# Convolution dealt out in program order, and its norm inside the mLSTM output stage

## The chip, the core and the metric

The kernel runs on one core of a Trainium2 chip. The metric is the device time of one launch in microseconds. Engines are named by their work: TensorE (PE in the rows, PEld for its weight loads), VectorE (DVE), ScalarE (ACT), GpSimd (POOL), SyncE (SP, which issues most transfers).

## What is computed

One layer of a diffusion backbone: 1024 latent tokens of width 1024, and 256 context tokens that share its weights. A first sub-layer mixes tokens in two groups of heads, a second one is a mixture of 64 experts. The change touches the first only. Cut to what matters:

```python
hx = modulate(rms_norm(x, g_pre_mix), shift, scale)         # hc likewise, of the context
z = h @ w_in + b_in                                          # q, k, v, o, gates, ga, gb
u = ga * sigmoid(gb)                                         # group B, convolution
hx_m = mlstm_bidir(q, k, v, gates, states_of_context)        # group A, chunks of 128 tokens
a = rms_norm_per_head(hx_m) * norm_g * sigmoid(o)
y = depthwise_conv(u, width=31, along rows of the grid) + conv_b
b = silu(layer_norm(y, ln_g, ln_b))                          # norm over 512 channels
x = x + gate * rms_norm(concat(a, b) @ w_out + b_out, g_post_mix)
x = x + gate2 * rms_norm(moe(modulate(rms_norm(x), ...)), g_post_ffn)
```

## The kernel before

Activations are kept with channels on the partitions: `X` holds 8 blocks of 128 channels by 1024 tokens. The modulated input is held as a high and a low half, `hH` and `hL`, of the same fp32r type, and each weight block likewise, `wfH` and `wfL`. A product is then three matmuls per block of 128 channels (`mm3`, L436 to L438). A split makes the two halves: a cast on ScalarE for the high one (L50) and a subtraction for the low one (L51), on VectorE or, where the call names it, on GpSimd.

The stages of the front, with the times of the profiled execution:

- To 63 us: the adaLN vectors, the modulation, and the first four features (`first`).
- 63 to 133 us: gate features for the convolution's input. `feat(t, j)` is 24 matmuls of 512 columns into a PSUM tile `pf` (4 buffers); `gated` turns two such features into one block of `U`, the first four blocks of `X`. `context` makes the context's sums of squares (L153, tile `va` as scratch) and its modulation between them.
- 133 to 199 us: the value and gate projections, 2 x 10 groups of 24 matmuls of 264 columns into `pv` (4 buffers), each evacuated by two VectorE additions (L348, L351). The weights `wvL` are split on GpSimd.
- 199 to 235 us: key features `kT`, and between them the steps of a generator, `gates`, which makes scans and transposes of the mLSTM's gate values; its last step turns `nata`, `natb` and `natc` into the columns `colW`, `colG` and `colF` by way of a PSUM tile with two buffers.
- 235 to 285 us: the chunk states (`states`), then `conv_norm`, the query features and the output gates (`o`, features 12 to 15), up to 328 us.
- 328 to 409 us: `outputs`, ten steps over eight chunks of 128 tokens. For a chunk: decay matrices (`pM`, ScalarE makes `Dm`), scores (`pQ`, VectorE multiplies `Dm` and `qs`), sums (`pN`, ScalarE copies to `hd`), division (`dn`, `hd`), a norm per head and transposes (`pH`). `filler` steps another generator, `ada`, between them; it computes the remaining adaLN vectors from weights that come by DMA (`wa`, `va`, `kT` as buffers) and splits the output weights (`woL`).
- From 409 us: the output projection, and the experts from about 530 to 1450 us.

The convolution (`conv`, L421 on) is four blocks of 31 VectorE instructions, called taps here: one multiplication by the middle weight (L425) and 30 multiply-adds over shifted rows (L431), each on 128 x 784 to 1008 elements, from `U` into `Y`, the last four blocks of `X`. Before, `later(LOW + 1000 * t)` gives them a low priority, and the scheduler puts them where VectorE has nothing else to do by its estimate. The last block is issued behind the key features.

`conv_norm` (L806 on) runs in two halves of 512 tokens: two additions over the four blocks (L813, L814), a product with ones for the mean (`pmu`, L816), a subtraction over four blocks (L817), squares on ScalarE (L820, L821), two additions (L822, L823), a product for the variance (`pva`, L826), a power on GpSimd (L830), a product that spreads the factor (`crs`, L833) and a multiplication over four blocks (L835). Then, for each block, a sigmoid of the scaled value (ScalarE, L838), the scaling (L839) and the product of both (L840).

The order of the other instructions is the program's, moved by a scheduler with priorities; `behind()` ties an instruction behind the last one issued on an engine.

Of the kernel before, what the change touches and what calls it, by code (L numbers as in the profile page):

```python
# [19 lines left out]
EPS = 1e-6  # L20
# [12 lines left out]
class Layer:  # L33
# [72 lines left out]
    def front(self, cp):  # L106
# [8 lines left out]
        gt = mix.tile([128, 10, 16], F32, name="gt")  # L115
# [199 lines left out]
        for t in range(4):  # L315
            if t in (1, 2):
                with self.behind():
                    context(t - 1)
            if t:
                for f, j in [(8 + t, 0), (8 + t, 1), (4 + t, 0), (4 + t, 1)]:  # L320
                    gated(t, f, j, feat(f, j))
# [62 lines left out]
        self.states(sp, stp, va, kT, cst, colW, acol)  # L384
# [18 lines left out]
        self.outputs(qT, kT, va, cst, colG, colF, rows, U)  # L403
# [17 lines left out]
    def conv(self, u, y, cw, cv):  # L421
        nc = self.nc
        u = u.rearrange("p (r w) -> p r w", w=ROW)
        y = y.rearrange("p (r w) -> p r w", w=ROW)
        nc.vector.tensor_scalar(y, u, cw[:, 15:16], cv[:, 0:1], op0=OP.mult, op1=OP.add)  # L425
        for i in range(CW):
            o = i - 15
            if o == 0:
                continue
            a, b = max(0, -o), min(ROW, ROW - o)  # L430
            nc.vector.scalar_tensor_tensor(y[:, :, a:b], u[:, :, a + o:b + o], cw[:, i:i + 1], y[:, :, a:b],  # L431
                                           op0=OP.mult, op1=OP.add)
# [8 lines left out]
    def gates(self, sp, pp, gt, colG, colF, colW, acol):  # L441
# [79 lines left out]
        for col, src, nm in ((colW, Ws, "a"), (colG, G, "b"), (colF, Fl, "c")):  # L521
            t = sp.tile([NR, 128], F32, name="nat" + nm)
            natural(t, src)
# [45 lines left out]
    def states(self, sp, pp, va, kT, cst, colW, acol):  # L569
# [4 lines left out]
        for c in range(9):  # L574
            for d in range(2):
# [22 lines left out]
                prev[d] = C  # L598

    def outputs(self, qT, kT, va, cst, colG, colF, rows, os):  # L600
# [101 lines left out]
        nxt, last, normed = products(0, decays(0)), None, None  # L702
        for x in range(10):
# [90 lines left out]
    def stage_mix(self, sp, X, j):  # L794
        fH = sp.tile([128, 8, 128], F32R, name="fH")
        fL = sp.tile([128, 8, 128], F32R, name="fL")
# [9 lines left out]
    def conv_norm(self, ys, cv):  # L806
        nc, tc = self.nc, self.tc
        sp, sp_ = self.pool("cn", 1)
        pp, pp_ = self.pool("cnp", 1, PSUM)
        for s in range(2):  # L810
            y = ys[:, :, s * 512:s * 512 + 512]
            a = sp.tile([128, 2, 512], F32, name="csa")
            nc.vector.tensor_tensor(a, y[:, :2], y[:, 2:], op=OP.add)  # L813
            nc.vector.tensor_tensor(a[:, 0], a[:, 0], a[:, 1], op=OP.add)  # L814
            pm = pp.tile([128, 512], F32, name="pmu")
            nc.tensor.matmul(pm, self.ones, a[:, 0], start=True, stop=True)  # L816
            nc.vector.scalar_tensor_tensor(y, pm.unsqueeze(1).to_broadcast([128, 4, 512]), -1.0 / 512, y,  # L817
                                           op0=OP.mult, op1=OP.add)
            sq = sp.tile([128, 2, 512], F32, name="csq")
# [4 lines left out]
            pv = pp.tile([128, 4], F32, name="pva")  # L824
            for j in range(4):
                nc.tensor.matmul(pv[:, j:j + 1], a[:, 0, j * 128:j * 128 + 128], self.ones[:, :1], start=True,  # L826
                                 stop=True)
            rc = sp.tile([128, 4], F32, name="crc", bufs=2)
            nc.vector.tensor_scalar(rc, pv, 1.0 / 512, EPS, op0=OP.mult, op1=OP.add)
            nc.gpsimd.tensor_tensor(rc, rc, self.mhalf[:, :4], op=OP.pow)  # L830
            rs = pp.tile([128, 512], F32, name="crs")
            for j in range(4):
                nc.tensor.matmul(rs[:, j * 128:j * 128 + 128], rc[:, j:j + 1].to_broadcast([128, 128]), self.ident,  # L833
                                 start=True, stop=True)
            nc.vector.tensor_tensor(y, y, rs.unsqueeze(1).to_broadcast([128, 4, 512]), op=OP.mult)  # L835
            for t in range(4):
# [4 lines left out]
        self.close(pp_)  # L841
        self.close(sp_)
# [989 lines left out]
```

## Time and profile before

| | us |
|---|---|
| median of three runs | 1489.70 |
| lowest, highest | 1486.15, 1490.43 |
| the profiled execution | 1489.12 |
| its span | 1487.3 |
| TensorE busy in it | 1414.0 (95%) |
| VectorE busy | 1126.0 (76%) |
| ScalarE busy | 753.6 (51%) |
| GpSimd busy | 482.8 (32%) |

A busy share is an average over stages with different limits, so the rows below are by stretch. A wait is listed as the engine that waited, the tile and line it waited at, and the engine, tile and line that released it. PEclk is the clock that TensorE was granted, as a share of its full one. Durations of consecutive instructions on one engine can overlap by some 70 ns.

### The profile page before, as it was taken

How to read it: one execution, taken by the hardware profiler on the slowest of the kernel's cores; microseconds unless marked ns; L12 is line 12 of the kernel's file. 1: busy time of each engine (PE TensorE's matmuls, PEld its weight loads, DVE VectorE, ACT ScalarE, POOL GpSimd, SP SyncE). 2: the span in 40 equal slices, each digit the busy share in tenths (PEclk: the TensorE clock that was granted, in tenths of full speed). 3: DMA queues.
4: the chain of work that ended last, by engine and by line, in shares of the span. 5: the costliest groups of instructions: out<-in, count | busy, mean ns of one | idle time of the engine just before them, and what ended most of it. 6: DMA issues, size and time to landing. Idle time of an engine off the chain costs nothing. (4 is left out here: it accounts for less than half of the span.)

```text
span 1487.3 us, 22926 instructions
## 1 busy us (share of the span) xinstructions
PE 1414.0 (95%) x8188; PEld 1085.2 (73%) x8195; DVE 1126.0 (76%) x1927; ACT 753.6 (51%) x1241; POOL 482.8 (32%) x322
## 2 busy tenths in 40 slices
PE   6999999998899989999999999999999999999975
PEld 4687987775577755866788888888777777777764
DVE  6899979767767896635578888888786877787636
ACT  4421011245533245535567676676676766676622
POOL 0245101112313331334333233333343354455324
PEclk9999999999999999999999999999999999999988
DMA  8421051018743577996999999999999999999975
GB/s 330 163 72 43 1 193 59 19 55 292 224 175 110 200 271 282 353 284 212 342 298 321 325 327 319 333 339 341 319 340 307 301 349 317 316 352 315 335 249 211
DMA packets 95409, 371.64 MB, mean 250 GB/s; under 512 B 18269, under 2 KB 28837, under 8 KB 68794
## 3 DMA queue, kind: packets, MB, share of 16 engines
q1 hardware_dynamic: 66970, 298.48, 53.7%
q0 software_dynamic: 26032, 70.19, 19.4%
q10 hardware_dynamic: 2288, 1.45, 0.4%
q8 instruction: 66, 1.08, 0.3%
q14 instruction: 53, 0.43, 0.1%
HBM read 322.38 MB, written 62.19 MB: 259 GB/s over the span
## 5 line engine op out<-in xcount | busy, mean ns | idle before, releaser
L51 DVE TENSOR_TENSOR u<-u,u 128x1024 fp32r<-128x1024 f32 x354 | 421.8, 1220 | 124.0 <-ACT u L50 97.3
L50 ACT CAST u<-u 128x1024 fp32r<-128x1024 f32 x354 | 361.3, 1052 | 107.6 <-PE pgu L438 41.6
L1580 POOL DMA_INDIRECT acc<-yb,dst x98 | 192.2, 1961 | 352.8 <-ACT hTH L50 118.4
L436 PE MATMUL pgu<-u,xH 128*128 128x512 f32 x608 | 246.9, 406 | 0.4
L437 PE MATMUL pgu<-u,xH 128*128 128x512 f32 x608 | 239.8, 394 | 0.0
L438 PE MATMUL pgu<-u,xL 128*128 128x512 f32 x608 | 239.2, 393 | 0.0
L1460 POOL DMA_INDIRECT xg<-hxd,tok x98 | 125.1, 1276 | 193.7 <-DVE rwj L1368 67.9
L431 DVE SCALAR_TENSOR_TENSOR X<-X,cw 128x912 f32<-128x912 f32 (+14 forms) x120 | 152.0, 1292 | 1.1
L436 PEld LDWEIGHTS pgu<-u,xH 128*128 128x128 f32 x608 | 115.0, 189 | 25.8 <-ACT u L50 2.6
L438 PEld LDWEIGHTS pgu<-u,xL 128*128 128x128 f32 x608 | 114.9, 189 | 24.9
L437 PEld LDWEIGHTS pgu<-u,xH 128*128 128x128 f32 x608 | 115.1, 189 | 21.7
L436 PE MATMUL py<-u,hTH 128*128 128x512 f32 x304 | 122.3, 402 | 0.5 <-ACT hTH L50 0.5
L437 PE MATMUL py<-u,hTH 128*128 128x512 f32 x304 | 119.9, 394 | 0.0
L438 PE MATMUL py<-u,hTL 128*128 128x512 f32 x304 | 118.6, 395 | 0.0
L437 PE MATMUL pf<-hL,wfH 128*128 128x512 f32 x256 | 103.6, 405 | 0.7 <-DVE hL L226 0.7
L51 DVE TENSOR_TENSOR xL<-px,xH 128x512 fp32r<-128x512 f32 x152 | 97.6, 682 | 7.6 <-ACT xH L50 7.2
L436 PE MATMUL pf<-hH,wfH 128*128 128x512 f32 x256 | 103.0, 406 | 0.0
L438 PE MATMUL pf<-hH,wfL 128*128 128x512 f32 x256 | 102.1, 399 | 0.0
L50 ACT CAST xH<-px 128x512 fp32r<-128x512 f32 x152 | 84.0, 593 | 14.7 <-PE pgu L437 8.7
L51 POOL TENSOR_TENSOR wfL<-wfr,wfH 128x1024 fp32r<-128x1024 f32 x14 | 48.9, 3493 | 117.3 <-ACT wfH L50 103.3
L1572 DVE COPY yb<-py 128x512 f32<-128x512 f32 x75 | 51.6, 688 | 46.3 <-PE py L438 45.8
L1482 PE MATMUL px<-ident,xg 128*128 128x128 f32 x600 | 83.7, 274 | 1.0 <-DVE nl L1265 1.0
(438 smaller groups left out, 2500.2 us busy)
## 6 DMA issues: line engine op xcount, KB each, us to landing
u<-in_we_dram SPq DMA_DIRECT2D x192, 1024.0 KB
wa<-in_wa_dram SPq DMA_DIRECT2D x40, 256.0 KB
wa<-in_wa_dram SPq DMA_DIRECT2D x8, 1024.0 KB
wfr<-in_wf_dram SPq DMA_DIRECT2D x16, 512.0 KB
v<-acc SPq DMA_DIRECT2D x16, 512.0 KB
acc<-zero SPq DMA_DIRECT2D x13, 512.0 KB
u<-in_ws_dram SPq DMA_DIRECT2D x6, 1024.0 KB
X<-in_xT_dram SPq DMA_DIRECT2D x8, 512.0 KB
```

What stands on the lines that cost most here:

```text
L50: self.nc.scalar.copy(H, src)
L51: return (eng or self.nc.vector).tensor_tensor(L, src, H.bitcast(F32), op=OP.subtract).ins
L431: nc.vector.scalar_tensor_tensor(y[:, :, a:b], u[:, :, a + o:b + o], cw[:, i:i + 1], y[:, :, a:b], op0=OP.mult, op1=OP.add)
L436: mm(out, lH, rH, start=start, stop=False, skip_group_check=free)
L437: mm(out, lH, rL, start=False, stop=False, skip_group_check=free)
L438: mm(out, lL, rH, start=False, stop=stop, skip_group_check=free)
L1460: nc.gpsimd.indirect_dma_start(out=x[:n], out_offset=None, in_=self.hx, in_offset=bass.IndirectOffsetOnAxis(ap=self.tok[:n, c:c + 1], axis=0),
L1482: nc.tensor.transpose(pt[:, k], x[:, (4 * q + k) * 128:(4 * q + k) * 128 + 128], self.ident)
L1572: nc.vector.tensor_copy(y[:, 512:], py)
L1580: nc.gpsimd.indirect_dma_start(out=self.acc[b % NA].rearrange("r (n d) -> (r n) d", n=n), in_=y[:rows], in_offset=None, out_offset=bass.In ...
```

## The change

1. **Taps.** `conv` becomes a generator that yields after each tap. A new `spend(n)` takes the next `n` taps of a list of such generators and keeps each in program order. It is called behind every gate feature (4 taps behind a first half; 3 or 2 behind a second), behind every value group (2), behind every key feature (4), behind every state step (1); the rest is spent behind the states.
2. **Splits.** The low halves of `wf` (all but two of its blocks were on GpSimd) and of `wv` are made on VectorE.
3. **PSUM of the value groups.** Odd groups use `pv` (4 buffers), even ones `pf` (4 buffers).
4. **Gates.** The generator yields once more, ahead of the transposes into `colW`, `colG`, `colF`; the first two query features stand ahead of that last step.
5. **The convolution's norm.** It leaves its place between the states and the query features and becomes a generator that `outputs` steps once per chunk, behind `divide(x, 0, pN)`. Chunks 0 and 2 take the sums, the mean and the subtraction of a half; chunks 1 and 3 its squares and variance; chunks 4 and 5 the spread factor and the multiplication; chunk 6 the activation. Its tiles take the buffers `fH` and `fL` that the output projection uses later, its products the PSUM tile `pH`, the factor the tile `gt`.
6. **Swish.** The sigmoid, the scaling and the product are one activation (Silu with scale and bias), four instructions of 128 x 1024, in place. The function table is loaded once more for it.

The diff's core:

```diff
-                self.split(wH, wL, wr, nc.gpsimd if len(wts) > 1 else None)
+                self.split(wH, wL, wr)
...
+        taps = []
+        def spend(n):
+            for _ in range(n):
+                while taps:
+                    ins = next(taps[0], None)
+                    if ins is not None:
+                        tc.keep_in_program_order(ins)
+                        break
+                    taps.pop(0)
+        taps.append(self.conv(U[:, 0], Y[:, 0], cw[:, 0], cv[:, 0]))
-        for t in range(4):
+        for t in range(1, 4):
...
-            if t < 3:
-                with self.later(LOW + 1000 * t):
-                    self.conv(U[:, t], Y[:, t], cw[:, t], cv[:, t])
+            for f, j in [(8 + t, 0), (8 + t, 1), (4 + t, 0), (4 + t, 1)]:
+                gated(t, f, j, feat(f, j))
+                spend((3 if t == 1 else 2) if j else 4)
+            taps.append(self.conv(U[:, t], Y[:, t], cw[:, t], cv[:, t]))
...
-                self.split(wH, wL, wr, nc.gpsimd)
+                self.split(wH, wL, wr)
...
-                ps = pv.tile([128, 264], F32, name="pv", bufs=4)
+                ps = pv.tile([128, 264], F32, name="pv", bufs=4) if j % 2 else pj.tile([128, 512], F32, name="pf", bufs=4)
+                ps = ps[:, :264]
...
+                spend(2)
...
-                if (t, j) >= (0, 2):
+                if (0, 2) <= (t, j) < (1, 2):
                     with self.behind():
                         next(gates, None)
-                    if (t, j) == (0, 2):
-                        with self.behind(mybir.EngineType.DVE), self.later(LOW):
-                            self.conv(U[:, 3], Y[:, 3], cw[:, 3], cv[:, 3])
+                spend(4)
...
+        query(0)
+        with self.behind():
+            next(gates, None)
-        self.states(sp, stp, va, kT, cst, colW, acol)
+        self.states(sp, stp, va, kT, cst, colW, acol, spend)
+        spend(CW * 4)
...
-        self.conv_norm(Y, cv)
-        for t in range(2):
-            for j in range(2):
-                nc.scalar.activation(qT[:, t, j * 512:j * 512 + 512], feat(t, j), AF.Identity, bias=bf[:, t:t + 1])
+        query(1)
...
+        swish = self.conv_norm(sp, pp, ys, cv)
         for x in range(10):
...
                 hs = [divide(x, 0, pN)]
+                next(swish, None)
...
-                g = sp.tile([128, 512], F32, name="csg", bufs=2)
-                nc.scalar.activation(g, y[:, t], AF.Sigmoid, scale=cv[:, t, 1:2], bias=cv[:, t, 2:3])
-                nc.vector.tensor_scalar(y[:, t], y[:, t], cv[:, t, 1:2], cv[:, t, 2:3], op0=OP.mult, op1=OP.add)
-                nc.vector.tensor_tensor(y[:, t], y[:, t], g, op=OP.mult)
+        self.grouped([lambda t=t: nc.scalar.activation(ys[:, t], ys[:, t], AF.Silu, scale=cv[:, t, 1:2],
+                                                       bias=cv[:, t, 2:3]) for t in range(4)])
```

The instructions that move, on VectorE. First where the context's sums (`va`) meet the first taps (`X<-X,cw`), behind the first gate features (`X<-pf,bf,X`). Before:

```order
L431 SCALAR_TENSOR_TENSOR X<-X,cw 128x16x50
L153 TENSOR_TENSOR va<-va 128x256
L431 SCALAR_TENSOR_TENSOR X<-X,cw 128x16x51
L214 TENSOR_SCALAR rc<-pc 128x2
L309 MEMSET va 128x40
```

Now:

```order
L233 SCALAR_TENSOR_TENSOR X<-pf,bf,X 128x512 x2
L153 TENSOR_TENSOR va<-va 128x256 x3
L214 TENSOR_SCALAR rc<-pc 128x2
L309 MEMSET va 128x40
L443 TENSOR_SCALAR X<-X,cw,cv 128x1024
```

The sums stand in one run, ahead of the first instruction of the convolution (L443).

The second place is the end of the gates' generator, where the columns are copied (`colW`, `colG`, `colF`) and the first key block is weighted (`kw`). Before:

```order
L514 TENSOR_SCALAR natc<-Fl 64x128
L515 TENSOR_SCALAR natc<-Fl 40x128
L431 SCALAR_TENSOR_TENSOR X<-X,cw 128x16x59
L526 COPY colW<-pc 128x104
L526 COPY colG<-pc 128x104
L431 SCALAR_TENSOR_TENSOR X<-X,cw 128x16x60
L526 COPY colF<-pc 128x104
L530 COPY acol<-pa 64x52 x2
L431 SCALAR_TENSOR_TENSOR X<-X,cw 128x16x61
L583 TENSOR_TENSOR kw<-pt,colW 128x256 x2
```

Now:

```order
L449 SCALAR_TENSOR_TENSOR X<-X,cw 128x16x53
L449 SCALAR_TENSOR_TENSOR X<-X,cw 128x16x54
L449 SCALAR_TENSOR_TENSOR X<-X,cw 128x16x55
L449 SCALAR_TENSOR_TENSOR X<-X,cw 128x16x56
L547 COPY colW<-pc 128x104
L547 COPY colG<-pc 128x104
L547 COPY colF<-pc 128x104
L51 TENSOR_TENSOR wfL<-wfr,wfH 128x1024
L551 COPY acol<-pa 64x52 x2
L604 TENSOR_TENSOR kw<-pt,colW 128x256 x2
```

Eight taps, four of them shown, now stand between the last row of `natc` and the copies, with a cast, two mask tiles and a split of weights among them; another split (`wfL`) follows the copies.

The third is the first chunk of the output stage, on VectorE. Before:

```order
L650 TENSOR_TENSOR qs_2715<-qT,pQ 128x256
L650 TENSOR_TENSOR qs_2720<-qT,pQ 128x256
L658 TENSOR_TENSOR Dm_2695<-Dm_2695,pQ 128x512
L658 TENSOR_TENSOR Dm_2703<-Dm_2703,pQ 128x512
L51 TENSOR_TENSOR woL<-wor,woH 128x512
L675 TENSOR_TENSOR dn<-hd_2774,colF 128x4
L677 SCALAR_TENSOR_TENSOR dn<-hd_2774,dn 128x4
L678 RECIPROCAL dn<-dn 128x4
L680 TENSOR_TENSOR hd_2774<-hd_2774,dn 128x4x128
```

Now:

```order
L672 TENSOR_TENSOR qs_2625<-qT,pQ 128x256
L843 SCALAR_TENSOR_TENSOR X<-pmu,X 128x4x512
L672 TENSOR_TENSOR qs_2630<-qT,pQ 128x256
L680 TENSOR_TENSOR Dm_2605<-Dm_2605,pQ 128x512
L680 TENSOR_TENSOR Dm_2613<-Dm_2613,pQ 128x512
L51 TENSOR_TENSOR woL<-wor,woH 128x512
L697 TENSOR_TENSOR dn<-hd_2684,colF 128x4
L699 SCALAR_TENSOR_TENSOR dn<-hd_2684,dn 128x4
L700 RECIPROCAL dn<-dn 128x4
```

The subtraction of the convolution's mean (L843) stands between the two multiplications of `qs`.

The last is ScalarE in the seventh chunk, where the decays of the last chunk (`Dm`) are followed by the copies of the sums (`hd<-pN`). Before:

```order
L637 ACTIVATE Dm_3499<-pM,colG 128x128 x4
L637 ACTIVATE Dm_3507<-pM,colG 128x128 x4
L50 CAST woH<-wor 128x512
L761 DMA ga_3686<-in_rows_dram 32x256
L673 COPY hd_3539<-pN 128x516
```

Now:

```order
L659 ACTIVATE Dm_3465<-pM,colG 128x128 x4
L864 ACT_TABLE_LOAD
L864 ACTIVATE X<-X,cv 128x1024 x3
L695 COPY hd_3497<-pN 128x516
L710 ACTIVATE hd_3441,ssq<-hd_3360 128x128 x4
```

The load of the function table and three of the four Silu (L864) stand ahead of the next copy of `hd`.

From the output projection on, the order on every engine is as before.

## Rows read from the trace of the kernel before

**Rows 1.** Windows by stretch: busy us (x instructions) of each engine, granted clock, DMA share.

```profile
63.00:328.20 265.20, 249.41 (x1450) 212.78 (x1449) 236.53 (x341) 55.30 (x80) 65.05 (x28) 0.97 0.18 58
328.20:409.20 81.00, 72.27 (x642) 45.90 (x649) 58.15 (x139) 45.85 (x154) 23.94 (x32) 0.94 0.80 262
530.00:1450.00 920.00, 905.63 (x5083) 687.77 (x5081) 669.74 (x1072) 574.53 (x868) 333.50 (x207) 0.99 0.94 315
```

**Rows 2.** TensorE's waits, 63 to 410 us: total us, times, longest us.

```profile
PE pv L436 <- DVE gt L351: 5.3, 1, 5.3
PE pc L525 <- DVE nata L515: 3.4, 1, 3.4
PE pmu L816 <- issue: 2.1, 1, 2.1
PE pc L213 <- DVE va L153: 2.0, 1, 2.0
PE crs L833 <- POOL crc L830: 2.0, 2, 1.7
...
PE pa L776 <- DMA kT<-in_wa_dram: 1.6, 1, 1.6
```

**Rows 3.** Windows within the value projections.

```profile
150.20:153.40 3.20, 2.87 (x13) 2.90 (x14) 3.20 (x5) 0.00 (x0) 0.00 (x0) 0.50 0.00 0
153.60:157.00 3.40, 3.40 (x30) 3.40 (x29) 3.40 (x8) 0.00 (x0) 0.00 (x0) 1.00 0.02 5
155.00:195.00 40.00, 39.65 (x326) 39.44 (x325) 39.82 (x57) 1.27 (x2) 4.05 (x2) 1.00 0.00 1
```

**Rows 4.** GpSimd's lines, 60 to 330 us: busy us, mean ns.

```profile
L51 POOL TENSOR_TENSOR wfL<-wfr,wfH 128x1024 fp32r<-128x1024 f32 x12 | 44.0, 3668 | 102.0 <-ACT wfH L50 88.0 <-DMA acc<-zero 14.0
```

**Rows 5.** VectorE's timeline in three places: start us, us, line, tile, count.

```profile
77.99 10.00 DVE L431 SCALAR_TENSOR_TENSOR X<-X,cw 128x896 f32<-128x896 f32 x5
...
142.64 5.50 DVE L431 SCALAR_TENSOR_TENSOR X<-X,cw 128x976 f32<-128x976 f32 x5
...
159.11 2.22 DVE L431 SCALAR_TENSOR_TENSOR X<-X,cw 128x928 f32<-128x928 f32 x2
...
161.66 2.21 DVE L431 SCALAR_TENSOR_TENSOR X<-X,cw 128x912 f32<-128x912 f32 x2
```

**Rows 6.** VectorE's lines, 63 to 330 us: busy us, mean ns.

```profile
L431 DVE SCALAR_TENSOR_TENSOR X<-X,cw 128x912 f32<-128x912 f32 (+14 forms) x120 | 152.0, 1292 | 1.1
...
L817 DVE SCALAR_TENSOR_TENSOR X<-pmu,X 128x2048 f32<-128x2048 f32 x2 | 4.6, 2288 | 1.6 <-PE pmu L816 1.6
L835 DVE TENSOR_TENSOR X<-X,crs 128x2048 f32<-128x2048 f32 x2 | 4.6, 2286 | 3.8 <-PE crs L833 3.8
...
L822 DVE TENSOR_TENSOR csa<-csa,csq 128x1024 f32<-128x1024 f32 x2 | 2.4, 1222 | 2.5 <-ACT csq L821 2.5
L813 DVE TENSOR_TENSOR csa<-X 128x1024 f32<-128x1024 f32 x2 | 2.4, 1220 | 0.0
...
L823 DVE TENSOR_TENSOR csa<-csa 128x512 f32<-128x512 f32 x2 | 1.4, 691 | 0.1
L814 DVE TENSOR_TENSOR csa<-csa 128x512 f32<-128x512 f32 x2 | 1.4, 685 | 0.0
```

**Rows 7.** TensorE's lines, 285 to 409 us.

```profile
L816 PE MATMUL pmu<-csa,ones 128*128 128x512 f32 x4 | 2.4, 685 | 2.1 <-issue 2.1
L833 PE MATMUL crs<-ident,crc 128*128 128x128 f32 x16 | 2.3, 288 | 2.0 <-POOL crc L830 2.0
```

**Rows 8.** ScalarE's timeline at the output stage's start and in its seventh chunk.

```profile
328.99 1.28 ACT L637 ACT_TABLE_LOAD   x1 [0.81 <-DVE X L398]
330.29 2.18 ACT L637 ACTIVATE Dm<-pM,colG 128x128 f32<-128x128 f32 x8
...
381.78 0.59 ACT L673 COPY hd<-pN 128x516 f32<-128x516 f32 x1 [3.69 <-PE pM L634]
```

**Rows 9.** ScalarE's line of the norm's squares, 200 to 330 us.

```profile
L820 ACT ACTIVATE csa<-X 128x1024 f32<-128x1024 f32 x2 | 2.1, 1057 | 0.6 <-DVE X L817 0.6
```

More of the change, by code (lines that the diff above doesn't have):

```diff
@@ L114, in front @@
         va = mix.tile([128, 10, NH, DV + 1], F32, name="va")
-        gt = mix.tile([128, 10, 16], F32, name="gt")
+        gt = self.gt = mix.tile([128, 10, 16], F32, name="gt")
         cw = mix.tile([128, 4, CW], F32, name="cw")
@@ L383, in front, with query @@
         qT = mix2.tile([128, 2, NX], F32, name="qT")
-        self.states(sp, stp, va, kT, cst, colW, acol)
+        def query(t):
+            for j in range(2):
+                nc.scalar.activation(qT[:, t, j * 512:j * 512 + 512], feat(t, j), AF.Identity, bias=bf[:, t:t + 1])
+        query(0)
[3 more added lines that the diff above has]
+        spend(CW * 4)
         self.masks(mix2)
@@ L401, in front @@
         self.close(pj_)
-        self.outputs(qT, kT, va, cst, colG, colF, rows, U)
+        self.outputs(qT, kT, va, cst, colG, colF, rows, U, Y, cv)
         self.close(rp_)
@@ L430, in conv @@
             a, b = max(0, -o), min(ROW, ROW - o)
[L431 to L432 removed]
+            yield nc.vector.scalar_tensor_tensor(y[:, :, a:b], u[:, :, a + o:b + o], cw[:, i:i + 1], y[:, :, a:b],
+                                                 op0=OP.mult, op1=OP.add)
     def mm3(self, out, lH, lL, rH, rL, start, stop, free=False):
@@ L520, in gates @@
             nc.sync.dma_start(self.rowd[i], t)
-        for col, src, nm in ((colW, Ws, "a"), (colG, G, "b"), (colF, Fl, "c")):
-            t = sp.tile([NR, 128], F32, name="nat" + nm)
-            natural(t, src)
+        nat = []
+        for src, nm in ((Ws, "a"), (G, "b"), (Fl, "c")):
+            nat.append(sp.tile([NR, 128], F32, name="nat" + nm))
+            natural(nat[-1], src)
+        yield
+        for col, t in zip((colW, colG, colF), nat):
             pc = pp.tile([128, 128], F32, name="pc", tag="s", bufs=2)
@@ L567, in bound_rows, with states @@
         return out
-    def states(self, sp, pp, va, kT, cst, colW, acol):
+    def states(self, sp, pp, va, kT, cst, colW, acol, spend):
         nc = self.nc
@@ L598, in states, with outputs @@
                 prev[d] = C
-    def outputs(self, qT, kT, va, cst, colG, colF, rows, os):
+                spend(1)
+    def outputs(self, qT, kT, va, cst, colG, colF, rows, os, ys, cv):
         nc, tc = self.nc, self.tc
@@ L794, in stage_mix @@
     def stage_mix(self, sp, X, j):
-        fH = sp.tile([128, 8, 128], F32R, name="fH")
-        fL = sp.tile([128, 8, 128], F32R, name="fL")
+        fH = sp.tile([128, 8, 128], F32R, name="fH", tag="fH")
+        fL = sp.tile([128, 8, 128], F32R, name="fL", tag="fL")
         self.split(fH, fL, X[:, :, j * 128:j * 128 + 128])
@@ L804, in project, with conv_norm @@
                 self.mm3(po[:, s], fH[:, k], fL[:, k], *self.wo[k, n], k == 0, k == 7)
[L806 to L812, printed above, removed]
+    def conv_norm(self, sp, pp, ys, cv):
+        nc = self.nc
+        mm = nc.tensor.matmul
+        halves = [ys[:, :, 512 * s:512 * s + 512] for s in range(2)]
+        bank = lambda nm: pp.tile([128, 512], F32, name=nm, tag="pH")
+        rc = self.gt[:, 0, :8].rearrange("p (s j) -> p s j", s=2)
+        for s, y in enumerate(halves):
+            a = self.spa.tile([128, 2, 512], F32, name="csa", tag="fH")
             nc.vector.tensor_tensor(a, y[:, :2], y[:, 2:], op=OP.add)
             nc.vector.tensor_tensor(a[:, 0], a[:, 0], a[:, 1], op=OP.add)
-            pm = pp.tile([128, 512], F32, name="pmu")
-            nc.tensor.matmul(pm, self.ones, a[:, 0], start=True, stop=True)
+            pm = bank("pmu")
+            mm(pm, self.ones, a[:, 0], start=True, stop=True)
             nc.vector.scalar_tensor_tensor(y, pm.unsqueeze(1).to_broadcast([128, 4, 512]), -1.0 / 512, y,
                                            op0=OP.mult, op1=OP.add)
-            sq = sp.tile([128, 2, 512], F32, name="csq")
+            yield
+            sq = self.spa.tile([128, 2, 512], F32, name="csq", tag="fL")
             nc.scalar.activation(a, y[:, :2], AF.Square)
@@ L823, in conv_norm @@
             nc.vector.tensor_tensor(a[:, 0], a[:, 0], a[:, 1], op=OP.add)
-            pv = pp.tile([128, 4], F32, name="pva")
+            pv = bank("pva")
             for j in range(4):
[L826 to L831, printed above, removed]
+                mm(pv[:, j:j + 1], a[:, 0, j * 128:j * 128 + 128], self.ones[:, :1], start=True, stop=True)
+            nc.vector.tensor_scalar(rc[:, s], pv[:, :4], 1.0 / 512, EPS, op0=OP.mult, op1=OP.add)
+            nc.gpsimd.tensor_tensor(rc[:, s], rc[:, s], self.mhalf[:, :4], op=OP.pow)
+            yield
+        for s, y in enumerate(halves):
+            rs = bank("crs")
             for j in range(4):
-                nc.tensor.matmul(rs[:, j * 128:j * 128 + 128], rc[:, j:j + 1].to_broadcast([128, 128]), self.ident,
-                                 start=True, stop=True)
+                mm(rs[:, j * 128:j * 128 + 128], rc[:, s, j:j + 1].to_broadcast([128, 128]), self.ident, start=True,
+                   stop=True)
             nc.vector.tensor_tensor(y, y, rs.unsqueeze(1).to_broadcast([128, 4, 512]), op=OP.mult)
-            for t in range(4):
-                g = sp.tile([128, 512], F32, name="csg", bufs=2)
-                nc.scalar.activation(g, y[:, t], AF.Sigmoid, scale=cv[:, t, 1:2], bias=cv[:, t, 2:3])
-                nc.vector.tensor_scalar(y[:, t], y[:, t], cv[:, t, 1:2], cv[:, t, 2:3], op0=OP.mult, op1=OP.add)
-                nc.vector.tensor_tensor(y[:, t], y[:, t], g, op=OP.mult)
-        self.close(pp_)
-        self.close(sp_)
+            yield
+        self.grouped([lambda t=t: nc.scalar.activation(ys[:, t], ys[:, t], AF.Silu, scale=cv[:, t, 1:2],
+                                                       bias=cv[:, t, 2:3]) for t in range(4)])
 NE, TK, DE = 64, 8, 256
```

5 lines of the change are left out of this document (1 added, 4 removed).

## The prediction

> **What bounds the kernel now.** I read the windows by stretch first, then TensorE's waits, then the lines and rows behind each wait. The windows [rows 1] show three stretches. From 530 to 1450 us, the experts, TensorE is busy 905.63 of 920.00 us. From 63.0 to 328.2, the front after its first loop, it is busy 249.41 of 265.20, and VectorE 236.53. From 328.2 to 409.2, the mLSTM output stage, TensorE is busy 72.27 of 81.00 and VectorE only 58.15. So the time is TensorE's own work plus its holes, and the holes before 409 are where an edit of this kind can act. Their list [rows 2] names VectorE or the convolution's norm behind most of them: 5.3 us on an evacuation of the value projections (gt, L351), 3.4 on the gate rows (nata), 2.1 and 2.0 in the norm (pmu, crs), 2.0 on the context's sums (va, L153). Each of the first three and the last is followed by a stretch at half clock. The one after the 5.3 us hole is shown: PEclk 0.50 from 150.2 to 153.4 with 13 matmuls, against 30 matmuls in the 3.4 us behind it at 1.00 [rows 3]. These are 1.2 and 2.4 GHz. Half the work in 3.2 to 3.4 us means that a hole of this sort costs 1.6 us more than its length.
>
> **The first gate features (63 to 79 us).** Before, the five sums of the context's squares stand between taps on VectorE, and GpSimd runs its splits of weights meanwhile (3668 ns each) [rows 4]. Taps that take 2.22 us for two at 159 take 10.00 us for five at 78 [rows 5], so the sums come late and TensorE waits 2.0 us. In the new order the sums stand in one block ahead of the first tap, and no split runs on GpSimd. I take the wait and its slow clock away: 2.0 + 1.6 = **3.6 us**. What comes late next is the weight splits, now VectorE's: 12 of 128x1024 in this stretch at the 1.22 us of a sum of that shape (L813) [rows 6], 14.6 us, and 8 of half that size, about 5 us by the same row (an estimate). Against these some 20 us stand the taps: 120 take 152.0 us, 1292 ns each [rows 6], and at the undisturbed 1.11 us of [rows 5] they would take 133. So the 20 us added and the 19 us saved nearly cancel. VectorE also loses the norm, so its 236.53 us must still fit into a front some 20 us shorter; they do, with little over.
>
> **The value projections (133 to 199 us).** One group of 24 matmuls takes TensorE 40.00 / 326 x 24 = 2.94 us [rows 3]. Two taps and an evacuation take VectorE 161.66 - 159.11 = 2.55 us [rows 5]. With two taps dealt out per group and eight PSUM buffers for four, VectorE keeps ahead. Before, VectorE ran five taps in a row from 142.64 on, 5.50 us [rows 5], while the four buffers were full; that hole of 5.3 us goes with its clock: 5.3 + 1.6 = **6.9 us**.
>
> **Gates and states (199 to 285 us).** Two query features now stand ahead of the transposes of the gate rows, so the 3.4 us on nata go, with 1.6 of clock: 5.0. A wait is added: the third transpose needs a PSUM buffer that the copy of colW frees, and that copy stands on VectorE behind eight taps, two mask tiles, a cast and a split. That is about 8 x 1.11 + 1.22 + 1 = 11.1 us (the last 1 my estimate from the smaller shapes), against two features on TensorE of about the same length. Queued behind it on TensorE are the rest of the query features and the states' transposes. I take 1.2 us; the ends are 0 and, with taps at 1.29 us, about 3. Net **3.8 us**.
>
> **The convolution's norm leaves the path between states and query features.** Its two waits go, 2.1 + 2.0, and 1.6 us of clock: **5.7 us**. Its matmuls (2.4 us, 2.3 us and sixteen of one column) [rows 7] go into the output stage at the same price, so they cancel. The 8 multiplications by scale and 8 by the sigmoid leave VectorE for good. The front gains 3.6 + 6.9 + 3.8 + 5.7 = **20.0 us**.
>
> **The output stage.** VectorE gets two subtractions and two multiplications over four blocks (2288 and 2286 ns) and the sums (2.4, 2.4, 1.4, 1.4 us in pairs) [rows 6], 16.8 us, of which the first sums, 1.9, run before the stage. It has 81.00 - 58.15 = 22.85 us of idle time, but its queue is in order and the chunk's chain (qs, Dm, dn, hd) runs through it. The ends are 0, all of it in idle time, and 14.9, all of it on the chain. The four long ones, 9.1 us, stand directly between links of that chain; I expose half of them, **4.6 us**, and leave the short sums hidden. On ScalarE, the squares take 4.2 us beside other work. The four Silu of 1024 elements come in the seventh chunk behind a load of the function table. A load took 1.28 us at 328.99, and the next activation began 0.02 us after it [rows 8]. With three Silu at the 1057 ns of a square of that size [rows 9], 4.5 us stand ahead of the next copy of hd. In that place that copy found ScalarE idle for 3.69 us at 381.78 [rows 8], so 0.8 us are left over; the ends are 0 and 4.5. **0.8 us.** Against this the stage's wait for kT's DMA, 1.6 us [rows 2], halves when chunks last longer: -0.8. The stage grows by 4.6 us beside the moved matmuls.
>
> The Trainium skill (ScalarE: Activation LUTs, What ACT_TABLE_LOAD costs) counts a drain of about 1.38 us beside the load of 1283 ns for each change of set. By that the stage would grow by 1.4 us more, an estimate, and the sum would end at 1475.1. No row here shows that drain: the one in [rows 8] goes on at once.
>
> **Sum.** 1489.1 (the profiled execution; its span is 1487.3) - 20.0 + 4.6 = 1473.7. The median of the three runs, 1489.7, lies 0.6 above that execution and the runs span 4.3. I stay with **1473.7**.
>
> **Rivals.** (A) VectorE's queue becomes the bound of the output stage and it is slower. The norm's matmuls stand in TensorE's order among the chunk's products, and each waits for its link on VectorE or ScalarE, so all 14.9 us of VectorE, 4.5 of Silu and 4.2 of squares are exposed: 23.6 against 20.0, **1492.7**. It decides when the holes of that stage grow from 8.7 us to over 28. Against it stand VectorE's idle 22.85 us; for it, that both engines would be over 85% full. (B) The taps in program order hold up what TensorE needs in the front. Eight splits of gate weights stand behind a tap of 1.11 us each, about 9 to 10 us of new holes: 1473.7 + 10 = **1484**. For it speaks that VectorE has little over; against it, the two-tap rhythm of [rows 5], which already keeps pace. (C) The stage takes the norm into its idle time, so neither the 4.6 nor the 0.8 appears: **1468**. (D) The gain is given back among the experts, whose weights come by DMA at a share of 0.94 [rows 1]: **1489**. Against it stands TensorE's busy 98% there, and 0.06 of 920 us, 55 us, in which the transfers could catch up.
>
> **How the numbers follow.** Chances: the forecast 0.50 (1470 to 1479), C 0.19, B 0.16, A 0.08, D 0.05, something else 0.02. The range reaches over C and most of B: 1466 to 1486; A, D and the tail of B stay outside, less than 2 in 10. A difference of 0.3%, 4.5 us, is about what a measurement of this kernel can tell from no change. Below 1485.2 lie the forecast, C and most of B: faster 0.83; within 0.3% D and the rest of B: 0.09; slower A: 0.08.
>
> **What would show it.** The list of TensorE's waits before the output stage should have none of the five named ones over 1.5 us, and PEclk should stay near 1.00 from 63 us to the stage. That stage should begin about 20 us earlier plus the length of the moved matmuls, near 301 to 305 us, and last 88 to 93 us. In it, waits on hd or on the norm's tiles of about 5 us in sum are mine, of 20 are A's. New waits on wfL or pf before 300 would be B's. The experts should take as long as before; if they take longer, D. I would be wrong first on how much of the four 2.29 us instructions the chunk chain feels.

## The result and the profile after

The changed kernel takes 1465.9 us (median of four runs, 1462.6 to 1466.7) against 1489.55 (four runs, 1486.2 to 1490.4). The ratio is 0.9846, with a 95% interval from 0.9827 to 0.9865. It is faster, as forecast, by 23.7 us where 16 were forecast. The time lies on the lower edge of the stated range, 1466 to 1486, 0.1 us below it in the median, and outside the forecast's own 1470 to 1479.

Windows of the changed kernel's profile (1466.07 us; span 1464.3), with the columns of [rows 1], by the same stretches of work: the front, the output stage, 920 us of experts. The columns are the window, its length, the busy us of TensorE, its weight loads, VectorE, ScalarE and GpSimd, the granted clock, the DMA share and GB/s.

```profile
63.00:303.20 240.20, 239.17 (x1426) 205.88 (x1425) 208.05 (x335) 47.37 (x72) 2.58 (x5) 1.00 0.20 64
303.20:388.20 85.00, 75.27 (x678) 49.37 (x684) 71.77 (x153) 55.13 (x163) 29.97 (x34) 0.96 0.76 249
509.00:1429.00 920.00, 906.60 (x5085) 689.07 (x5084) 670.66 (x1070) 573.63 (x867) 332.88 (x208) 0.99 0.94 315
```

In the front TensorE is busy 239.17 of 240.20 us, and its granted clock is 1.00; before it was 249.41 of 265.20 at 0.97 [rows 1]. In the output stage VectorE went from 58.15 of 81.00 us to 71.77 of 85.00. The experts are as before. TensorE's waits of the changed kernel over 63 to 388 us, columns of [rows 2]:

```profile
PE pH L720 <- DVE X L862: 2.9, 1, 2.9
PE pa L800 <- DMA wa<-in_wa_dram: 2.5, 2, 2.3
PE pa L800 <- DMA va<-in_wa_dram: 1.4, 2, 1.2
...
PE pM L653 <- ACT X L414: 0.8, 1, 0.8
```

None of the five named holes of [rows 2] is left. All of the waits shown fall in the output stage; the 0.8 us on pM stand ahead of its first matmul. Where the time went is read from the starts of the same matmuls in both timelines (start, duration): the first feature, the first value group, the output stage (pM), the output projection (po) and the first expert (pgu). First before, then after.

```profile
29.60 0.50 PE L436 MATMUL pf<-hH,wfH 128*128 128x512 f32 x1
...
133.37 0.28 PE L436 MATMUL pv<-wvH,hH 128*128 128x264 f32 x1
...
199.34 0.40 PE L436 MATMUL pf<-hH,wfH 128*128 128x512 f32 x1
...
328.23 0.38 PE L631 MATMUL pM<-cm,idb 128*128 128x512 bf16 x1 [0.78 <-ACT X L397]
...
408.93 0.50 PE L436 MATMUL po<-woH,fH 128*128 128x512 f32 x1
...
531.87 0.59 PE L1492 MATMUL pgu<-u,xR 128*128 128x512 f32 x1
```

```profile
32.55 0.50 PE L454 MATMUL pf<-hH,wfH 128*128 128x512 f32 x1
...
132.82 0.28 PE L454 MATMUL pf<-wvH,hH 128*128 128x264 f32 x1
...
191.26 0.40 PE L454 MATMUL pf<-hH,wfH 128*128 128x512 f32 x1
...
303.16 0.38 PE L653 MATMUL pM<-cm,idb 128*128 128x512 bf16 x1 [0.78 <-ACT X L414]
...
388.17 0.50 PE L454 MATMUL po<-woH,fH 128*128 128x512 f32 x1
...
509.80 0.59 PE L1515 MATMUL pgu<-u,xR 128*128 128x512 f32 x1
```

| stretch | before | after | difference |
|---|---|---|---|
| to the first feature | 29.60 | 32.55 | +2.95 |
| first feature to value groups | 103.77 | 100.27 | -3.5 |
| value groups | 65.97 | 58.44 | -7.5 |
| keys to output stage | 128.89 | 111.90 | -17.0 |
| output stage | 80.70 | 85.01 | +4.3 |
| projection to first expert | 122.94 | 121.63 | -1.3 |
| the rest of the span | 955.4 | 954.5 | -0.9 |

The first line of the table is no part of the change: the first feature starts between 29.6 and 32.6 us in the fourteen profiles, whose kernels differ only behind it. From the first feature to the output stage 28.0 us are gone. Part of that is the norm's matmuls, which went into the stage (2.4, 2.3 and 1.9 us by their busy times before, 6.6 in sum; in a row they take less, since they overlap).

### The profile page after: what moved, and what is told of

It is laid out like the page before. It is cut to its first block, busy times and chain, and to the rows that moved or that the text cites. A ratio compares the mean times of both kernels' runs of the same rounds, so it can differ in the third digit from the quotient of the medians.

```text
span 1464.3 us, 22838 instructions
## 1 busy us (share of the span) xinstructions
PE 1405.1 (96%) x8188; PEld 1080.2 (74%) x8195; DVE 1109.2 (76%) x1933; ACT 753.3 (51%) x1238; POOL 421.5 (29%) x300
## 5 line engine op out<-in xcount | busy, mean ns | idle before, releaser
L449 DVE SCALAR_TENSOR_TENSOR X<-X,cw 128x784 f32<-128x784 f32 (+14 forms) x120 | 137.4, 1145 | 1.6
L455 PE MATMUL pf<-hL,wfH 128*128 128x512 f32 x256 | 100.5, 393 | 0.0
L50 ACT CAST xH<-px 128x512 fp32r<-128x512 f32 x152 | 84.0, 592 | 14.6 <-PE pgu L455 8.7
L1539 ACT ACTIVATE sgu<-pgu 128x256 f32<-128x256 f32 x79 | 30.5, 386 | 103.2 <-PE pgu L456 103.2
```

Of the source, the lines that this page charges most:

```text
L50: self.nc.scalar.copy(H, src)
L449: yield nc.vector.scalar_tensor_tensor(y[:, :, a:b], u[:, :, a + o:b + o], cw[:, i:i + 1], y[:, :, a:b], op0=OP.mult, op1=OP.add)
L455: mm(out, lH, rL, start=False, stop=False, skip_group_check=free)
L1539: nc.scalar.activation(sg, pg[:, :DE], AF.Silu)
```

## Experiments

Times are medians of four or more runs, with the ratio to the kernel before on the same chip and its 95% interval. The chips differ: the kernel before takes 1486.9, 1488.2 and 1489.7 us on the three of the experiments, so between sections the ratios compare better than the times. "Changed" is the changed kernel, 0.9846 (0.9827 to 0.9865).

**Norm back in the front.**

```diff
+        self.conv_norm(Y, cv)          # ahead of query(1), in the form of before
         query(1)
...
-                next(swish, None)
```

> The changed kernel with the convolution's norm back between the states and the second pair of query features, in its old form (sigmoid, scaling, product); everything else as changed. Theory 1 (the output stage takes the norm into its idle time, so that only its matmuls cost there): the two waits and the slow clock come back, about 5.7 us, and the stage falls from 85 to 81 us: about 1471.5. Theory 2 (the forecast's: the four long VectorE instructions and the Silu cost the stage 4.6 us more than the matmuls): about 1467, and the stage falls to 76 to 77 us.

Measured: 1492.5, ratio 1.0018 (1.0001 to 1.0035). Both theories were wrong, by over 20 us. Its waits from 192 to 335 us:

```profile
PE pva L849 <- DVE csa L846: 8.1, 1, 8.1
PE crs L856 <- POOL crc L853: 3.4, 2, 1.7
PE pmu L839 <- DVE csa L837: 2.8, 1, 2.8
PE pmu L839 <- issue: 2.8, 1, 2.8
PE pM L654 <- DVE X L858: 2.4, 1, 2.4
...
317.00:339.00 22.00, 9.78 (x49) 6.17 (x52) 17.39 (x25) 9.43 (x13) 1.40 (x1) 0.50 0.48 169
```

The norm's chain is exposed for 19.5 us, and in all of 317 to 339 us, where the hole of 8.1 us lies, the granted clock is 0.50 and TensorE is busy 9.78 of 22.00 us. Both theories had priced the norm's return by the waits of the kernel before, which are not those of this front. The output stage itself is 82.7 us here.

**Norm alone moved, the rest as before.**

```diff
 # the kernel before, with only:
-        self.conv_norm(Y, cv)          # ahead of the query features
...
+                next(swish, None)      # in the output stage, with Silu
```

> The kernel before with only the norm moved into the output stage and its sigmoid replaced by Silu. Theory 1: the front loses the waits pmu and crs and one slow stretch, 5.7 us, and the stage grows by the matmuls it takes over: about 1484, with the waits on the value projections (5.3) and on nata (3.4) still there. Theory 2: 4.6 us of it are lost again in the stage: about 1488.5.

Measured: 1481.2, 0.9945 (0.9926 to 0.9965): 8.5 us gained, more than theory 1 said. Its stage is 83.6 us with the norm, 80.7 before without: the 2.9 us are less than the matmuls' 6.6. The stretch from the keys to the stage takes 117.0 us (201.16 to 318.18), 11.9 less than before. The holes on gt, nata (3.4) and va (2.0) are still there:

```profile
PE pv L435 <- DVE gt L351: 6.4, 1, 6.4
```

**Splits back on GpSimd.**

```diff
-                self.split(wH, wL, wr)
+                self.split(wH, wL, wr, nc.gpsimd if len(wts) > 1 else None)
...
-                self.split(wH, wL, wr)
+                self.split(wH, wL, wr, nc.gpsimd)
```

> The changed kernel with the low halves of the front's weights split on GpSimd again. If GpSimd's splits stretched the taps beside them, the 120 taps take 150 us again instead of 137, about 13 us more, while VectorE loses 20 us of splits; TensorE then waits again in the first gate features, about 2 us with 1.6 of slow clock: about 1469 to 1470. If it was the order alone (sums ahead of the taps) that took the wait away: no change, 1466, with the taps slower all the same.

Measured: 1470.9, 0.9884 (0.9856 to 0.9911), 5.0 us above changed. The size was right and the place was not: there is no wait on va, the taps take 1329 ns each, and TensorE waits later, where the gates end:

```profile
PE pc L546 <- DVE colW L547: 5.4, 1, 5.4
```

**Four buffers for the value groups.**

```diff
-                ps = pv.tile([128, 264], F32, name="pv", bufs=4) if j % 2 else pj.tile([128, 512], F32, name="pf", bufs=4)
-                ps = ps[:, :264]
+                ps = pv.tile([128, 264], F32, name="pv", bufs=4)
```

> The changed kernel with all value groups in the four buffers of pv. If the second set of buffers is what removed the 5.3 us hole, a hole of 3 to 5 us with its slow clock comes back: 1470 to 1473. If dealing the taps out two per group is enough by itself: 1466, and no wait over 1 us in the value projections.

Measured: 1467.6, 0.9862 (0.9837 to 0.9887), not told apart from changed. The value groups take the same 58.3 us from first to last matmul and have no wait.

**Last step of the gates ahead of the query features.**

```diff
-        query(0)
         with self.behind():
             next(gates, None)
+        query(0)
```

> The changed kernel with the last step of the gates (the transposes of nata, natb, natc) ahead of the first two query features again. If those features are what covers the wait on nata, a hole of about 3.4 us with 1.6 us of slow clock comes back: about 1471. If the dealt-out taps already let VectorE reach nata in time: about 1466, with no wait over 1 us at the transposes.

Measured: 1466.0, 0.9854 (0.9817 to 0.9892): no change. The waits at the transposes are small without the cover:

```profile
PE pc L546 <- DVE colW L547: 0.9, 1, 0.9
```

**Taps as low-priority fill again.**

```diff
-                        tc.keep_in_program_order(ins)
...
+        def low(t):
+            with self.later(LOW + 1000 * t):
+                list(self.conv(U[:, t], Y[:, t], cw[:, t], cv[:, t]))
...
-            taps.append(self.conv(U[:, t], Y[:, t], cw[:, t], cv[:, t]))
+            if t < 3:                  # the last block behind the key features, as before
+                low(t)
```

> The changed kernel with the convolution's instructions as low-priority fill again, as before, instead of dealt out in program order; splits on VectorE, eight buffers, the order of the gates and the norm in the output stage stay. If dealing out is what removes the holes: the 5.3 us hole of the value projections comes back, smaller for the second set of buffers, and the context's sums stand between taps again, 2.0 us, each with its slow clock: 1472 to 1478. If the splits' new engine and the buffers did it: 1466 to 1468.

Measured: 1465.8, 0.9850 (0.9818 to 0.9882). Dealing the taps out gains nothing in this kernel; no wait on va or gt came back.

**Fill and four buffers together.** Both edits above.

> Two parts undone at once: the convolution's instructions are low-priority fill again, and all value groups use the four buffers of pv; splits on VectorE, the order of the gates and the norm's place stay. Undone singly, neither brought the hole of the value projections back. If each of the two removes it by itself, it comes back here, 4 to 6 us and 1.6 of slow clock: 1471 to 1474. If neither matters and it was the splits on GpSimd that caused it: 1465 to 1467.

Measured: 1464.3, 0.9838 (0.9813 to 0.9862). The second expectation held, to 0.7 us (1465 to 1467 was said): neither matters while the splits are on VectorE. Fill, four buffers and GpSimd's splits were together in the kernel with the norm alone moved, which has the 6.4 us hole; here there is none in the value groups.

**Fill and GpSimd's splits together.**

> Two others undone at once: low-priority fill, and the splits on GpSimd; eight buffers, the order of the gates and the norm's place stay. If GpSimd's splits caused the holes of the front where the taps are fill: the wait of 2.0 us on va and its slow clock come back, and one of some us in the value projections: 1471 to 1476. If eight buffers cover that: about 1471, as with the splits alone undone.

Measured: 1480.7 (1475.1 to 1484.5), 0.9938 (0.9918 to 0.9958), 13 us by the ratios above the same kernel with the splits on VectorE (16 above the one with four buffers, measured on the same chip), and above the 1471 to 1476 that was expected. Eight buffers keep the value groups free of a long hole, though the splits are on GpSimd and the taps are fill; the delay turns up around them, at the context's sums, at the padded gates and at their columns:

```profile
PE pc L553 <- DVE colW L554: 4.8, 1, 4.8
PE pg L490 <- DVE pad L482: 2.7, 1, 2.7
PE pc L213 <- DVE va L153: 2.0, 1, 2.0
...
PE pf L462 <- POOL wvL L51: 0.7, 1, 0.7
```

Behind the waits on pad and colW the matmuls run at half clock again (0.50 from 213.9 to 217.0 us); behind the one on va the granted clock is 1.00 (74.9 to 78.3).

**Norm back in the front, taps as fill.**

> The norm back in the front in its old form, and the taps as low-priority fill; splits on VectorE, eight buffers and the order of the gates stay. If dealing out is what made the norm's return cost 26 us (the last tap comes late, and the norm's chain behind it finds no features left to cover it), this kernel is at 1471 to 1476. If the chain is exposed because the shortened front and the early query features leave too little to cover it, wherever the taps stand: 1485 to 1493.

Measured: 1475.05, 0.9904 (0.9880 to 0.9928): 17 us below the first experiment, which differs in the dealing-out alone, and within the 1471 to 1476 of its first expectation. The longest waits:

```profile
PE crs L863 <- POOL crc L860: 2.4, 2, 1.7
PE pmu L846 <- issue: 2.4, 1, 2.4
```

The norm's first sum (csa, line of before L813) starts at 281.96 us here and at 296.00 with the taps dealt out. VectorE's timeline of both, around the last tap; first as fill, then dealt out:

```profile
267.55 0.48 DVE L583 MEMSET rw<- 80x512 f32 x1
...
274.48 1.03 DVE L457 SCALAR_TENSOR_TENSOR X<-X,cw 128x784 f32<-128x784 f32 x1
...
281.51 0.42 DVE L579 TENSOR_TENSOR rwR<-rw,rwR 32x256 fp32r<-32x256 f32 x1 [4.74 <-ACT rwR L578]
281.96 1.22 DVE L843 TENSOR_TENSOR csa<-X 128x1024 f32<-128x1024 f32 x1
...
281.58 0.48 DVE L576 MEMSET rw<- 80x512 f32 x1
...
286.07 1.03 DVE L450 SCALAR_TENSOR_TENSOR X<-X,cw 128x784 f32<-128x784 f32 x1
...
295.54 0.42 DVE L572 TENSOR_TENSOR rwR<-rw,rwR 32x256 fp32r<-32x256 f32 x1 [4.75 <-ACT rwR L571]
296.00 1.23 DVE L836 TENSOR_TENSOR csa<-X 128x1024 f32<-128x1024 f32 x1
```

The sum does not start behind the last tap, which ends 6.5 and 8.9 us earlier. It starts behind the split of two tiles of rows that the kernel reads back from memory (rwR), and that waits 4.7 us in both kernels for ScalarE's copy, which waits for a DMA into rw (3.7 and 5.0 us). The first of these transfers is issued behind the clearing of rw on VectorE (268.1 and 282.1 us), and the clearing stands among the taps: dealt out, it comes 14.0 us later, as the sum does. A kernel with the norm ahead of these rows was not run.

**Six more long VectorE instructions in the output stage.**

```diff
                 next(swish, None)
+                if x < 6:
+                    e = ys[:, :, 512:] if x in (0, 1, 4) else ys[:, :, :512]
+                    nc.vector.scalar_tensor_tensor(e, e, 1.0, e, op0=OP.mult, op1=OP.max)
```

> The changed kernel with one more VectorE instruction over 128 x 4 x 512 elements, about 2.3 us, in each of the first six chunks of the output stage: it multiplies a half of the convolution's result by 1 and changes nothing; 13.7 us in all. Theory 1 (VectorE has room in the stage): the stage grows by at most 3 us beyond 85, and the time is under 1469. Theory 2 (half of a long instruction is felt): 6.9 us, 1473. Rival A of the prediction (the chunk's chain feels all of it): 13 to 14 us, 1479 to 1480.

Measured: 1475.2 (runs from 1466.7 to 1480.7), 0.9916 (0.9885 to 0.9948): 9.3 us above changed. In the profile the stage grows from 85.0 to 91.0 us. Its window:

```profile
301.70:392.70 91.00, 77.18 (x679) 49.46 (x684) 82.51 (x156) 54.68 (x162) 33.76 (x34) 0.94 0.71 234
```

VectorE is busy 82.51 of 91.00 us. So the next 13.7 us are felt by about half or more (6.0 in the profile, 9.3 by the medians, with a wide spread), though the changed stage has 85.00 - 71.77 = 13.23 us of VectorE's idle time, which would just hold them, and though the norm's own were felt little.

**The norm's products copied out of PSUM by ScalarE.**

```diff
+            nc.scalar.copy(a[:, 1], pm)
-            nc.vector.scalar_tensor_tensor(y, pm..., -1.0 / 512, y, op0=OP.mult, op1=OP.add)
+            nc.vector.scalar_tensor_tensor(y, a[:, 1:]..., -1.0 / 512, y, op0=OP.mult, op1=OP.add)
...
+            nc.scalar.copy(b[:, 0], rs)
-            nc.vector.tensor_tensor(y, y, rs..., op=OP.mult)
+            nc.vector.tensor_tensor(y, y, b..., op=OP.mult)
```

> The changed kernel with the two products of each half of the norm that VectorE reads from the PSUM tile pH (the mean and the spread factor) copied to SBUF by ScalarE first, so that the tile is free for the next transposes after 0.6 us instead of after VectorE's 2.3 us. If TensorE's wait on pH behind the multiplication (2.9 us with 1.7 us of slow clock in the changed kernel) came from the held tile, it goes and the time falls by 3 to 5 us, to 1461 to 1463; if it came from VectorE's load as such, the wait turns up at another tile and the time stays within 1 us.

Measured: 1465.9, 0.9850 (0.9818 to 0.9882): no change. The 2.9 us on pH are gone, and others came:

```profile
PE pN L687 <- DVE Dm L680: 3.3, 3, 1.9
...
PE pQ L646 <- DVE Dm L680: 1.0, 1, 1.0
```

**The same, with the long instructions cut into four.**

```diff
+            for t in range(4):
+                nc.vector.scalar_tensor_tensor(y[:, t], a[:, 1], -1.0 / 512, y[:, t], op0=OP.mult, op1=OP.add)
...
+            for t in range(4):
+                nc.vector.tensor_tensor(y[:, t], y[:, t], b[:, 0], op=OP.mult)
```

> The kernel with the copies of the norm's products to SBUF, and the two long VectorE instructions of each half cut into four of 128 x 512, so that links of the chunk's chain can go between them. If single blocks of 2.3 us on the chain cause the waits on Dm that took the place of the wait on pH (4.3 us), the stage falls from 84 to about 80 us and the time to 1461 to 1463. If VectorE's load in the stage is what counts (the pieces take 2.8 us for 2.3), nothing falls: 1465 to 1468.

Measured: 1463.0 (1461.8 to 1467.5), 0.9835 (0.9806 to 0.9864). The waits on Dm fell from 4.3 us to 0.4, and the last sums of the stage (pN) start 81.2 us after its beginning, against 84.2 in the changed kernel. The time is 2.9 us lower with overlapping intervals; it is not shown to beat the changed kernel. The Trainium skill (Perfetto Trace Analysis, Optimizing Scalar/DVE Operations) says that where VectorE isn't full but causes bubbles on others, breaking up instructions may let work complete sooner; the waits on Dm agree, the time leaves it open.

## Why the prediction was right, and where it was not

**The direction and the bound** held: TensorE's holes in the front were what could be had, and of 15.79 us of idle time there 1.03 are left; the output stage keeps its own, 9.73 us for 8.73. The stage began at 303.2 us (301 to 305 was said), no wait of the five is over 1.5 us, and the front's granted clock is 1.00. The runs close the account: with the norm alone moved the ratio is 0.9945; with the buffers and the gates' order added it is 0.9938 (the kernel with fill and GpSimd's splits), no difference that can be told; with the splits on VectorE too it is 0.9850, the changed kernel's. Dealing the taps out adds nothing to that.

**First gate features, 3.6 us: measured 3.5.** Size right. The prediction gave two reasons, the order of the sums and GpSimd's splits; either alone is enough. With the splits back but the taps dealt out there is no wait on va, nor with the taps as fill and the splits on VectorE; with both undone its 2.0 us return, there without the half clock that the forecast added.

**Value groups, 6.9 us: measured 7.5, for half of the reason.** The prediction put it down to two taps per group and eight buffers. Both undone together cost nothing once the splits are on VectorE. The hole is there where fill, four buffers and GpSimd's splits meet: 5.3 us in the kernel before, 6.4 with the norm alone moved. It goes with the splits' move alone, which the prediction did not count here, and it goes with the eight buffers alone. Whether the two taps per group would do it alone was not run. That [rows 5] shows two taps and an evacuation in 2.55 us held, but it is a row of a stretch where GpSimd was not splitting.

**Gates, 3.8 us, and norm, 5.7 us: measured 17.0 less the norm's matmuls**, at most 6.6, so at least 10.4 for 9.5. The kernel with the norm alone moved has 11.9 of the 17.0, at least 5.3 without the matmuls for the norm's 5.7; 5.1 are left for the gates' 3.8. The added wait on colW, priced at 1.2 us, did not occur; the early query features were not needed either.

**Splits for taps, priced at nearly nothing.** This is the term that failed worst, though its sum was right: some 20 us of splits were forecast and 19 us saved on taps. VectorE's lines of the changed kernel, 60 to 310 us (busy, mean ns):

```profile
L449 DVE SCALAR_TENSOR_TENSOR X<-X,cw 128x784 f32<-128x784 f32 (+14 forms) x120 | 137.4, 1145 | 1.6
L51 DVE TENSOR_TENSOR wfL<-wfr,wfH 128x1024 fp32r<-128x1024 f32 x12 | 14.6, 1218 | 1.1 <-ACT wfH L50 1.1
...
L51 DVE TENSOR_TENSOR wvL<-wvr,wvH 128x528 fp32r<-128x528 f32 x8 | 5.5, 702 | 0.3 <-ACT wvH L50 0.3
```

The taps fell from 1292 to 1145 ns, 14.6 us by these lines, and the four multiplications that open a block from 7.4 to 3.2 us; the splits added 20.1. VectorE has little less to do (with the edit and the taps as fill its last tap comes 6 us earlier, 243.5 against 249.4 us behind the first feature), and yet this edit is worth 13 to 16 us with the taps as fill and 5 with them dealt out. The waits show where: what TensorE waits for came late (2.0 + 2.7 + 4.8 us, two stretches at half clock behind them). An even trade on VectorE was taken for an even trade on the path; what counts is which instruction is late. Why the backlog always meets those three places was not taken apart further.

**Output stage, 4.6 us beside the matmuls: measured 4.3 with them.** "I expose half of them" failed. Without the norm the stage takes 80.7, 82.7 and 80.5 us (the kernel before and the two with the norm back in the front); with it, in the eight profiles whose norm is the changed kernel's, 81.4 to 89.3, 84.1 in the mean. About 3 us, less than the matmuls' 6.6, is the price of the whole norm, by means of profiles that spread by 8. The stage is shorter than the 88 to 93 us that were said, and the wait on the norm's tiles is 2.9 us of about 5. So rival C is nearer there: most of the norm's 15 us went into VectorE's 22.85 idle us. Of the next 13.7, into 13.23 idle us, about half is felt: the factor was right for a second load of that size and wrong for the first. Why the limit lies between them is not shown. The Silu block, priced at 0.8 us, stayed hidden. ScalarE's timeline in that chunk:

```profile
371.02 1.28 ACT L864 ACT_TABLE_LOAD   x1
372.69 3.50 ACT L864 ACTIVATE X<-X,cv 128x1024 f32<-128x1024 f32 x3 [0.39 <-DVE X L862]
376.85 0.59 ACT L695 COPY hd<-pN 128x516 f32<-128x516 f32 x1 [0.65 <-PE pN L689]
```

The load takes 1.28 us again, the activation ahead of it ends at 371.01 us, and the next one waits 0.39 us behind its end for VectorE's result; the copy of hd behind it waited 0.65 us for TensorE. By the Trainium skill (ScalarE: Activation LUTs, What ACT_TABLE_LOAD costs) the prediction had estimated 1.4 us of drain beside the load. It is not seen here, ahead of the load or behind it.

**The sum.** From the keys to the output projection, where the matmuls' move drops out, 17.0 - 4.3 = 12.7 us went; the forecast had 3.8 + 5.7 - 4.6 = 4.9. This difference, 7.8 us, is the whole miss of the sum: the 4.6 us of the stage and the 1.2 of colW did not come, and the last 2.0 are not assigned. Elsewhere 0.6 in the value groups, 1.3 in the projection (the granted clock of its first 41 us is 1.00, before 0.96) and 0.9 behind it were gained beyond the forecast, 0.1 less was gained in the first gate features, and the later start of this profile took 2.95 back.

**Rivals.** A did not come, the stage's holes being 9.73 us and not over 28, but its mechanism did, in the front of the first experiment: with the norm there, its matmuls stood in TensorE's order and waited 19.5 us for their links. B did not come: ahead of the stage no wait on wfL or pf is over 0.2 us. The 5.4 us on colW with the splits on GpSimd are not B's, since with the taps as fill they are 4.8. C, 1468 at a chance of 0.19, lies nearest to the time; the range reached this far down only to take in C. D did not come: TensorE is busy 906.60 of 920 us among the experts at the same DMA share, 0.94.

## What to carry to other kernels

When several edits close the same holes, undo them in pairs too: dealing the taps out changed nothing singly, and undone together with the splits' move it brought 13 to 16 us back, against 5 for the splits alone. The price of a chain depends on what stands ahead of its first link in the engine's order: the norm cost 8 to 11 us in the front with the taps as fill, and about 26 with them dealt out, where an instruction ahead of it waited for a transfer that the taps had put off by 14 us. Before a share of added work is charged to the path, look at how much idle time the engine has in that stage, but do not take it for a rule: 15 us into 22.85 idle ones cost about 3 with the norm's matmuls, and 13.7 into 13.23 cost 6 or more.

## What the runs showed of the hardware

Beside GpSimd's subtraction of two SBUF tiles some of VectorE's instructions take longer, others do not. VectorE's lines with the splits on GpSimd (fill), then on VectorE, 30 to 320 and 30 to 310 us:

```profile
L456 DVE SCALAR_TENSOR_TENSOR X<-X,cw 128x912 f32<-128x912 f32 (+14 forms) x120 | 150.6, 1281 | 1.1
L226 DVE SCALAR_TENSOR_TENSOR hL<-X,sh,hH 128x512 fp32r<-128x512 f32 x16 | 13.7, 887 | 1.3 <-ACT hH L225 0.3
L224 DVE SCALAR_TENSOR_TENSOR X<-X,gs,rs 128x512 f32<-128x512 f32 x15 | 10.6, 744 | 0.2
...
L450 DVE TENSOR_SCALAR X<-X,cw,cv 128x1024 f32<-128x1024 f32 x4 | 7.4, 1845 | 0.0
```

```profile
L226 DVE SCALAR_TENSOR_TENSOR hL<-X,sh,hH 128x512 fp32r<-128x512 f32 x16 | 11.5, 747 | 0.7
L224 DVE SCALAR_TENSOR_TENSOR X<-X,gs,rs 128x512 f32<-128x512 f32 x16 | 11.2, 742 | 1.6 <-PE rs L219 1.5
...
L443 DVE TENSOR_SCALAR X<-X,cw,cv 128x1024 f32<-128x1024 f32 x4 | 3.2, 799 | 0.0
```

The taps (1281 against 1145 ns), the differences hL (887, 747) and the sums va (574, 421) read two SBUF tiles and are stretched. The modulation (744, 742), of the same size as hL, reads one operand from PSUM (rs) and is not, but only two of its instructions ran beside a split (1.41 us for both, as elsewhere). Two tiles are not the whole condition: the multiplication that opens a block of the convolution (1845, 799) reads one SBUF tile and is stretched most, and so is the scaling of the output gates (`X<-X,ng`), which takes 2.40 us beside a split and 0.76 without one (307.97):

```profile
286.43 2.39 POOL L51 TENSOR_TENSOR wfL<-wfr,wfH 128x1024 fp32r<-128x1024 f32 x1 [14.77 <-ACT wfH L50]
...
286.98 2.40 DVE L422 TENSOR_SCALAR X<-X,ng 128x1024 f32<-128x1024 f32 x1 [3.96 <-ACT X L421]
```

It ends 0.56 us behind the split. The two hL that ran beside a split (45.73 and 47.29) and the multiplication at 109.12 end 0.54 to 0.55 us behind theirs: they did not share the time of the split, they finished behind it. The Trainium skill (SBUF — State Buffer, SBUF: two separate sides) says that a VectorE instruction with two SBUF inputs contends with GpSimd's reads for a shared pair of ports, held for a whole instruction; the two hL agree.

A split takes VectorE 1218 ns. On GpSimd the mean of 3668 [rows 4], which the prediction took for the time of each, hides a wide spread: of the fourteen in the kernel before the median is 2497 ns, the longest 13636.
